# Dilated queries, keys and half of the gate tiles as 2x2 block products in a hybrid encoder layer

## The chip, the core and the metric

The kernel runs on one core of a Trainium2 chip. The core has a matrix engine (TensorE, in the profile PE, with its weight loads as PEld), a vector engine (VectorE, DVE), an engine for activations (ScalarE, ACT), GpSimd (POOL) and SyncE (SP), from whose queue all DMAs of this kernel are issued. Matrix products are summed in PSUM, eight banks of 128 x 512 numbers; all else on the chip lies in SBUF. GpSimd works on SBUF alone. The metric is the device time of one execution in microseconds (us), as the median of several runs; a profile is taken of one execution of its own.

## The reference

One layer of a bidirectional encoder, 1024 tokens of width 1024, all in float32. A normalized input is multiplied by one wide matrix, and the result is cut into the inputs of two attention branches and of their gates:

```python
h = rmsnorm(x, attn_norm_g)
proj = h @ w_in
(c_q, c_kv, k_rope, z_mla, q_dil, k_dil, v_dil, z_dil,
 g_mla, g_dil) = jnp.split(proj, split_points, axis=-1)
a_out = mla_attention(c_q, c_kv, k_rope, positions, mla_q_norm_g, mla_kv_norm_g, w_uq, w_ukv)
y_mla = (a_out * jax.nn.silu(z_mla)) @ w_o_mla
d_out = dilated_mixture(q_dil, k_dil, v_dil, positions)
y_dil = (d_out * jax.nn.silu(z_dil)) @ w_o_dil
gate_mla = jax.nn.sigmoid(g_mla + b_gate[:D_MODEL])
gate_dil = jax.nn.sigmoid(g_dil + b_gate[D_MODEL:])
merged = gate_mla * y_mla + gate_dil * y_dil
return x + merged @ w_out
```

The first branch is latent attention with 8 heads over all keys. The second has three groups of 8 heads with dilations 1, 4 and 16; its queries and keys (3 x 512 columns of `w_in` each) are rotated by position, every query sees the keys up to 64 steps of its dilation away, and the groups are mixed by their softmax denominators. A last RMSNorm follows.

## The kernel before

Every large product is made in three passes: each operand is split into a rounded high part and the remaining low part, and `mm3` (lines 67 to 71) issues high x high, high x low and low x high into the same bank. So a product of a 128 x 128 weight tile with 512 tokens is three matmuls. `split` (73 to 76) makes the high part on ACT and the low part on the engine it is given. The input, transposed to channels by tokens, stays in SBUF as `hT_h` and `hT_l` (8 x 128 channels by 1024 tokens), and `R` holds the factor of each token's norm.

The work is staged. First come the latents and, with 256 columns at a time, the dilated values (`dil_v`). Then `dil_qk` computes queries and keys of the dilated branch, once for each of 3 groups, 2 quads of heads and query or key: two tiles of 128 weight columns (first and second halves of four heads' dimensions), for each half of the tokens 2 x 8 x 3 matmuls into two of six banks, then `rope` (four DVE products, one difference and one sum on POOL), high parts on ACT and low parts on POOL, and stores to DRAM by head, component and part. Group 1 stores the tokens rearranged by residue of 4, group 2 by residue of 16.

Attention follows, first dilated (`dil_attention`), then latent (`mla_attention`). Both leave TensorE waiting for softmax, so other products are put between as fillers: `fillers` is a generator in which every step is one `mm3`. It goes through 24 tiles of the branch gates (0 to 7) and merge gates (8 to 23), 16 steps a tile, then the pieces `brd` of the dilated result, the dilated output projection (64 steps), and, as soon as the first three of four pairs of latent heads are done, the latent output projection (3 steps a piece, 16 pieces). `feed(n)` takes n steps on average at its place, the rates are in `FEED`: the first six are for dilated attention, the last two for latent attention, where they stand twice and four times in a double block of queries. Nineteen steps run ahead of attention (`FIRST_FEED`). What the generator has not done of the latent output projection by the end of attention (all pieces not in `early`) is done in `output`, which adds the last pair of heads, merges the two branches, splits the result, loads and splits `w_out`, and multiplies.

The tile framework places the buffers and waits, and orders each engine's instructions by a simulated schedule of its own, in which a filler is held behind the instruction that `feed` names. The lines that matter most here:

```python
            for i in [4, 5, 6, 7, 0, 1, 2, 3, *range(16, 24), *range(8, 16)]:
                w = self.wtile(a["wt"][T_ZM + i])
...
        while todo:
            while todo[0][0] >= self.mla_done:
                yield
...
                        self.feed(FEED[6])
...
                        self.feed(FEED[7])
```

## Time and profile before

| | |
|---|---|
| median of 3 runs | 1328.5 us (1323.28 to 1333.44) |
| the profiled execution's own time | 1329.38 us |
| its span | 1327.2 us |
| TensorE busy | 1272.2 us (96%) |
| VectorE, ScalarE, GpSimd busy | 647.8, 563.5, 455.3 us |
| mean granted TensorE clock | 0.983 |

A line of a group reads: source line, engine, operation, output and inputs by the program's names, their shapes, the count; then the busy time of all and the mean duration of one in ns; then the idle time of the engine before them and what ended it. The duration of a matmul contains its way through the array, in which the next one already runs, so groups of matmuls look longer than the time that they take from the engine. A table by stretches gives the busy time of each engine with the number of its instructions, then the granted clock, the share of the DMA engines and GB/s. A row of the timeline starts with its time in the span and its duration; in brackets stands the idle time before it and what ended that.

### The profile page before, as it was taken

The page shows a single profiled execution, that of the slowest core. Times are in us where ns is not written, and L with a number is a line of the kernel's source. Part 1 is how long each engine was busy: PE and PEld are TensorE (multiplying, and loading weights), DVE is VectorE, ACT ScalarE, POOL GpSimd, SP SyncE. Part 2 cuts the span into 40 slices and gives each one's busy share as a digit, 9 for nine tenths or more (in the row PEclk, how much of TensorE's full clock was granted, in tenths as well). Part 3 has the DMA queues.
Part 4 walks back from the last instruction along what each step waited for, and adds up shares of the span by engine and source line. Part 5 has one row for each costly group of instructions (what it writes and reads, how often), then busy time and mean ns, then how long its engine had stood idle before and what let it go on. Part 6 is the DMA issues. An engine that isn't in the chain of part 4 may idle for free.

```text
span 1327.2 us, 19295 instructions
## 1 busy us (share of the span) xinstructions
PE 1272.2 (96%) x7101; PEld 1106.5 (83%) x7101; DVE 647.8 (49%) x1204; ACT 563.5 (42%) x1102; POOL 455.3 (34%) x302
## 2 busy tenths in 40 slices
...
GB/s 321 225 163 295 194 238 111 144 212 153 112 110 155 134 111 155 159 188 223 192 186 209 200 211 189 173 106 160 95 92 108 104 178 121 61 123 210 128 93 77
DMA packets 128254, 213.04 MB, mean 161 GB/s; under 512 B 36440, under 2 KB 65696, under 8 KB 126304
## 3 DMA queue, kind: packets, MB, share of 16 engines
...
## 4 chain that ended last, share of the span: by engine, by line
PE 69%; DMA 9%; DVE 6%; issue 2%; SPq 1%; ACT 1%; POOL 0%; DVEq 0%; ACTq 0%; POOLq 0%
PE pj L69 17%; PE pj L71 16%; PE pj L70 16%; PE pt L543 4%; PE av L551 2%; PE av L552 2%; PE s_mla L69 2%; PE s_mla L70 2%; PE s_mla L71 2%; DMA s_sd<-av_t 2%; PE pt L642 1%; PE av L663 1%; SPq L65 1%; PE s_ps L698 1%; PE s_ps L634 1%
## 5 line engine op out<-in xcount | busy, mean ns | idle before, releaser
L76 POOL TENSOR_TENSOR w_l<-w_raw,w_h 128x1024 fp32r<-128x1024 f32 (+1 forms) x70 | 167.5, 2396 | 440.3 <-ACT w_h L75 390.3
L69 PE MATMUL pj<-hT_h,w_h 128*128 128x512 f32 x768 | 314.5, 410 | 2.2 <-DVE zg_z L428 2.1
L71 PE MATMUL pj<-hT_h,w_l 128*128 128x512 f32 x768 | 301.9, 393 | 0.0
L70 PE MATMUL pj<-hT_l,w_h 128*128 128x512 f32 x768 | 301.2, 392 | 0.0
L233 DVE TENSOR_TENSOR rope_m<-pj,cs_d 128x512 f32<-128x512 f32 x96 | 61.8, 686 | 241.1 <-PE pj L71 236.5
L76 DVE TENSOR_TENSOR pt_l<-pt,pt_h 128x512 fp32r<-128x512 f32 x192 | 131.4, 686 | 91.5 <-ACT pt_h L75 89.4
L71 PEld LDWEIGHTS pj<-hT_h,w_l 128*128 128x128 f32 x768 | 145.0, 189 | 31.6
L69 PEld LDWEIGHTS pj<-hT_h,w_h 128*128 128x128 f32 x768 | 145.5, 189 | 27.6 <-DVE zg_z L428 3.0
L75 ACT CAST pt_h<-pt 128x512 fp32r<-128x512 f32 x192 | 112.0, 584 | 130.3 <-PE pt L543 62.1
L70 PEld LDWEIGHTS pj<-hT_l,w_h 128*128 128x128 f32 x768 | 145.8, 190 | 24.6
L70 PE MATMUL pj<-w_l,hT_h 128*128 128x256 f32 x384 | 109.1, 284 | 0.0
L71 PE MATMUL pj<-w_h,hT_l 128*128 128x256 f32 x384 | 108.9, 284 | 0.0
L69 PE MATMUL pj<-w_h,hT_h 128*128 128x256 f32 x384 | 108.9, 284 | 0.0
L75 ACT CAST w_h<-w_raw 128x1024 fp32r<-128x1024 f32 (+1 forms) x70 | 72.3, 1034 | 73.9 <-PE pj L70 59.4
L529 DVE TENSOR_REDUCE m_nm<-s_mla 128x1 f32<-128x1024 f32 x64 | 78.0, 1220 | 33.2 <-PE s_mla L71 33.1
L608 ACT ACTIVATE p<-p,d_st 128x256 f32<-128x256 f32 x128 | 64.4, 504 | 58.5 <-DVE d_st L607 58.5
L532 ACT ACTIVATE p<-s_mla,m_nm 128x1024 f32<-128x1024 f32 x64 | 71.8, 1122 | 25.4 <-PE pt L543 18.4
L543 PE MATMUL pt<-consts,p 128*128 128x128 f32 x512 | 79.7, 276 | 1.8 <-ACT p L532 1.8
L69 PEld LDWEIGHTS pj<-w_h,hT_h 128*128 128x128 f32 x384 | 73.7, 192 | 1.1
L70 PEld LDWEIGHTS pj<-w_l,hT_h 128*128 128x128 f32 x384 | 73.7, 192 | 0.8
L71 PEld LDWEIGHTS pj<-w_h,hT_l 128*128 128x128 f32 x384 | 73.5, 191 | 0.7
L607 DVE CUSTOM_DVE_ANT_0 p<-s_ps,masks 128x256 f32<-128x256 f32 x128 | 51.1, 417 | 45.9 <-PE s_ps L635 25.2
...
## 6 DMA issues: line engine op xcount, KB each, us to landing
w_raw<-wt SPq DMA_DIRECT2D x48, 512.0 KB, 4.4
op_b<-s_dq SPq DMA_DIRECT2D x32, 512.0 KB, 8.6
...
w_raw<-wv SPq DMA_DIRECT2D x12, 512.0 KB, 6.3
```

The lines of the kernel that those rows point to most:

```text
L69: mm(out, lh, rh, start=start, stop=False)
L70: mm(out, lh, rl, start=False, stop=False)
L71: return mm(out, ll, rh, start=False, stop=stop)
L75: self.nc.scalar.copy(out=h, in_=raw)
L76: sub.tensor_tensor(out=l, in0=raw, in1=h.bitcast(F32), op=ALU.subtract)
L233: v.tensor_tensor(out=mi, in0=p, in1=tab, op=ALU.mult)
L529: v.tensor_reduce(out=nm[:, hh, qb:qb + 1], in_=s, axis=AX.X, op=ALU.max, negate=True)
L532: nc.scalar.activation(out=p, in_=s, func=AF.Exp, bias=nm[:, hh, qb:qb + 1], accum_out=den[:, hh, qb:qb + 1])
L543: self.anchor = nc.tensor.transpose(pt[:, o:o + 128], P[b2][:, 128 * kc:128 * kc + 128], self.ident)
L551: nc.tensor.matmul(a_out, vv[:, kc], ph[:, s], start=kc == 0, stop=False)
L607: nc.vector.tensor_tensor_reduce(out=p, in0=s, in1=mask, op0=ALU.add, op1=ALU.min, scale=-0.125, scalar=3e38, accum_out=nm)
L608: nc.scalar.activation(out=p, in_=p, func=AF.Exp, scale=-1.0, bias=nm, accum_out=den)
```

## The change

For two tiles of weight columns, the product over 1024 channels and 1024 tokens is cut into 2 x 2 blocks (two column tiles, two halves of the channels, two halves of the tokens) and made with seven block products instead of eight, in Winograd's form of Strassen's scheme. Each block product is 4 x 3 matmuls of 512 tokens.

- `block_sums` loads the input again and makes, once, four sums and differences of its blocks, split into high and low parts (8 tiles of 8 KB per partition, kept until the last product).
- `block_loads`, `block_minus`, `block_operand`: the two raw weight tiles are loaded two pairs ahead; POOL makes four differences of weight blocks in place; each of the seven blocks is split (ACT, POOL) five products ahead of its use (`LEAD`).
- `block_product` adds into four banks a, b, c, d; c, d and a get a second product. `block_steps` says at which product each further step is issued: copies of banks on ACT, sums of banks on DVE in PSUM, then the rotation, now wholly on DVE with the result in PSUM, high parts on ACT, low parts on DVE, and stores by head and half of the tokens.
- `blocks` runs 16 pairs: the 12 of queries and keys, and 4 of the merge gates 8 to 15 at the places that `ZG_PAIRS` gives. Inside `manual_schedule` every engine keeps the order of the source. All eight banks are used, four for each of two pairs in turn.
- The fillers lose the gate tiles 8 to 15, and the last two rates of `FEED` go from 1.1 to 0.7.
- Queries and keys are stored as head, component, row, part, token, with rows of 512 tokens a store; the loads follow this, keys with two DMAs instead of one, and group 1's keys are read in two runs of 128 columns. `wtile` and `dil_v` hold split weights in halves, four buffers instead of two. The multiplication of the rotary tables by `R` and the zero stores move ahead of the block stage.

```diff
-FEED = (1.9, 1.35, 1.2, 1.25, 2, 3, 1.1, 1.1)
+FEED = (1.9, 1.35, 1.2, 1.25, 2, 3, 0.7, 0.7)
+LEAD = 5
+ZG_PAIRS = ((8, 2), (10, 5), (12, 8), (14, 11))
...
+    def block_sums(self, sp, tp):
+        nc, a = self.nc, self.a
+        p = nc.gpsimd
+        self.sh = [sp.tile([128, 4, 512], F32R, name=f"s{i}_h") for i in range(4)]
+        self.sl = [sp.tile([128, 4, 512], F32R, name=f"s{i}_l") for i in range(4)]
+        for kc in range(4):
+            y = {}
+            for i in range(2):
+                for k in range(2):
+                    x = y[i, k] = tp.tile([128, 512], F32, name=f"y{i}{k}", bufs=2)
+                    c = kc + 4 * k
+                    self.dma(x, a["xt"][i, :, c])
+                    nc.scalar.mul(x, x, self.ga[:, c:c + 1])
+            p.tensor_tensor(out=y[1, 1], in0=y[1, 0], in1=y[1, 1], op=ALU.add)
+            p.tensor_tensor(out=y[1, 0], in0=y[0, 0], in1=y[1, 0], op=ALU.subtract)
+            p.tensor_tensor(out=y[0, 0], in0=y[1, 1], in1=y[0, 0], op=ALU.subtract)
+            p.tensor_tensor(out=y[0, 1], in0=y[0, 1], in1=y[0, 0], op=ALU.subtract)
+            for i, x in enumerate((y[1, 1], y[0, 0], y[1, 0], y[0, 1])):
+                self.split(x, self.sh[i][:, kc], self.sl[i][:, kc], nc.vector)
+    def block_loads(self, n, item):
+        raw = [self.raw_pools[n % 2].tile([128, 8, 128], F32, name="w_raw", bufs=2) for _ in range(2)]
+        for i in range(2):
+            self.dma(raw[i], self.a["wt"][item[0] + i])
+        self.blk[n] = {(k, i): raw[i][:, 4 * k:4 * k + 4] for k in range(2) for i in range(2)}
+    def block_minus(self, j, items):
+        n, k = divmod(j, 7)
+        if n < len(items) and k in (2, 3, 4, 6):
+            b = self.blk[n]
+            out, x, y = {2: ((0, 0), (0, 1), (0, 0)), 3: ((0, 1), (1, 1), (0, 1)), 4: ((0, 0), (1, 1), (0, 0)), 6: ((1, 0), (1, 0), (0, 0))}[k]
+            self.nc.gpsimd.tensor_tensor(out=b[out], in0=b[x], in1=b[y], op=ALU.subtract)
+    def block_operand(self, j, items):
+        n, k = divmod(j, 7)
+        if n < len(items):
+            wp = (self.wp, self.wpx)[j % 2]
+            h = wp.tile([128, 4, 128], F32R, name="w_h", bufs=4)
+            l = wp.tile([128, 4, 128], F32R, name="w_l", bufs=4)
+            self.split(self.blk[n][((0, 0), (1, 0), (0, 0), (0, 1), (0, 0), (1, 1), (1, 0))[k]], h, l, self.nc.gpsimd)
+            self.opd[j] = h, l
+    def block_product(self, j, ps):
+        k = j % 7
+        hx = lambda i, c: tuple(x[:, 4 * c:4 * c + 4, 512 * i:512 * i + 512] for x in (self.hTh, self.hTl))
+        act = (lambda: hx(0, 0), lambda: hx(0, 1), lambda: self.s[0], lambda: self.s[2], lambda: self.s[1], lambda: self.s[3], lambda: hx(1, 1))[k]()
+        w = self.opd.pop(j)
+        out = ps["abcdacd"[k]]
+        for kc in range(4):
+            self.mm3(out, w[0][:, kc], w[1][:, kc], act[0][:, kc], act[1][:, kc], k < 4 and kc == 0, k in (1, 4, 5, 6) and kc == 3, skip=True)
+    def block_steps(self, n, item, ps, tp):
+        nc = self.nc
+        v, act = nc.vector, nc.scalar
+        a, b, c, d = (ps[x] for x in "abcd")
+        tmp = {}
+        def copied(i, x):
+            tmp[i] = tp.tile([128, 512], F32, name="st_c", bufs=2)
+            act.copy(out=tmp[i], in_=x)
+        def both():
+            tmp["t"] = tp.tile([128, 512], F32, name="st_t")
+            v.tensor_tensor(out=tmp["t"], in0=d, in1=tmp[1], op=ALU.add)
+        add = lambda x, i: v.tensor_tensor(out=x, in0=x, in1=tmp[i], op=ALU.add)
+        steps = {
+            2: [lambda: copied(0, a)],
+            3: [lambda: add(b, 0)],
+            4: [lambda: copied(1, c)],
+            5: [both],
+            6: [lambda: copied(2, a), lambda: add(a, "t")],
+            7: [lambda: add(c, 2)],
+            9: [lambda: add(d, 2)],
+        }
+        put = lambda k, f: steps.setdefault(k, []).append(f)
+        if item[1] is None:
+            first = item[0] - T_ZM
+            def out(half, i, x):
+                z = tp.tile([128, 512], F32, name=f"rope_m{i}")
+                t = tp.tile([128, 512], F32, name=f"dq_st{i}{half}")
+                self.zg_out(first + i, half, x, z, t)
+            for k, half, i, x in ((8, 0, 0, b), (8, 0, 1, c), (10, 1, 0, d), (11, 1, 1, a)):
+                put(k, lambda half=half, i=i, x=x: out(half, i, x))
+            return steps
...
+        def rope(half, pa, pb):
+            c512 = slice(half * 512, half * 512 + 512)
+            cos, sin = self.cos_d[:, c512], self.sin_d[:, c512]
+            m = []
+            def sines():
+                for i, x in enumerate((pb, pa)):
+                    m.append(tp.tile([128, 512], F32, name=f"rope_m{i}"))
+                    v.tensor_tensor(out=m[i], in0=x, in1=sin, op=ALU.mult)
+            def cosines():
+                for x in (pa, pb):
+                    v.tensor_tensor(out=x, in0=x, in1=cos, op=ALU.mult)
+            def sums():
+                v.tensor_tensor(out=pa, in0=pa, in1=m[0], op=ALU.subtract)
+                v.tensor_tensor(out=pb, in0=pb, in1=m[1], op=ALU.add)
+            return sines, cosines, sums
...
+        def high(half, o):
+            tiles(half)
+            for i in range(2):
+                x, y = views(half, i, o[i])
...
+        def low(half, o):
+            if g < 2:
+                for i in range(2):
+                    x, y = views(half, i, o[i])
+                    v.tensor_tensor(out=y[1], in0=x, in1=y[0].bitcast(F32), op=ALU.subtract)
+        def store(half):
+            for i in range(2):
+                for j in range(4):
+                    x = slice(32 * j, 32 * j + 32)
+                    if g < 2:
+                        self.dma(dst[j, i, :, :, off + 512 * half:off + 512 * half + 512], st[i, half][x])
+                    elif half:
+                        self.dma(dst[j, i, :, 0], st[i, 0][x])
+        r0, r1 = rope(0, b, c), rope(1, d, a)
+        put(7, r0[0])
+        put(8, r0[1])
+        put(8, r0[2])
+        put(9, r1[0])
+        put(10, lambda: high(0, (b, c)))
+        put(10, r1[1])
+        put(11, r1[2])
+        put(11, lambda: low(0, (b, c)))
+        put(12, lambda: high(1, (d, a)))
+        put(12, lambda: store(0))
+        put(12, lambda: low(1, (d, a)))
+        put(13, lambda: store(1))
+        return steps
+    def blocks(self, items, tp, pp):
...
+        places = 7 * len(items)
+        steps, ps = {}, {}
+        for n in range(2):
+            self.block_loads(n, items[n])
+        for j in range(LEAD):
+            self.block_minus(j, items)
+            self.block_operand(j, items)
+        self.block_minus(LEAD, items)
+        with self.tc.manual_schedule():
+            for x in range(1, places + 14):
+                n, k = divmod(x - 1, 7)
+                j = x - 1
+                if j < places:
+                    if k == 0:
+                        ps[n] = {c: pp.tile([128, 512], F32, name=f"st_{c}{n % 2}") for c in "abcd"}
+                        steps[n] = self.block_steps(n, items[n], ps[n], tp)
+                    self.block_product(j, ps[n])
+                todo = []
+                for m, y in ((n, k + 1), (n - 1, k + 8)):
+                    if m in steps:
+                        todo += steps[m].pop(y, [])
+                for f in todo:
+                    f()
+                self.block_operand(j + LEAD, items)
+                self.block_minus(j + LEAD + 1, items)
+                if k == 2 and n + 2 < len(items):
+                    self.block_loads(n + 2, items[n + 2])
...
-            for i in [4, 5, 6, 7, 0, 1, 2, 3, *range(16, 24), *range(8, 16)]:
+            for i in [4, 5, 6, 7, 0, 1, 2, 3, *range(16, 24)]:
...
-            self.dma(q[rows], self.dq[g][h].rearrange("p c r t -> (c r) p t"))
-        self.dma(k[:, :S + pad], self.dk[g][h].rearrange("a c r t -> (a c r) t"))
+            self.dma(q[rows], self.dq[g][h].rearrange("c r p t -> (c r) p t"))
+        for p in range(2):
+            self.dma(k[64 * p:64 * p + 64, :S + pad], self.dk[g][h].rearrange("c r p t -> p (c r) t")[p])
...
-                qs = slice(128 * b, 128 * b + 128)
-                ks = slice(128 * b, 128 * b + 256) if g == 0 else slice(256 * u, 256 * u + 256)
+                if g == 0:
+                    qs, kb = slice(128 * b, 128 * b + 128), k[:, 128 * b:128 * b + 256]
+                else:
+                    qs, kb = slice(512 * i + 128 * u, 512 * i + 128 * u + 128), k[:, :S].rearrange("p (x r m) -> p r x m", x=2, r=4)[:, u]
...
-            self.dq = [dt(f"s_dq{g}", (8, 2 if g < 2 else 1, 2, 32, S), F32R if g < 2 else F32) for g in range(3)]
+            self.dq = [dt(f"s_dq{g}", (8, 2, 32, 2 if g < 2 else 1, S), F32R if g < 2 else F32) for g in range(3)]
...
-                                for quad in range(2):
-                                    self.dil_v(g, quad, vp, pj)
-                    nc.vector.memset(z, 0.0)
+                            self.dil_v(0, 0, vp, pj)
+                            self.dil_v(0, 1, vp, pj)
+                    sp = sums.enter_context(tc.tile_pool(name="sums", reuse_waits="tile", bufs=1))
+                    with tc.tile_pool(name="bs", reuse_waits="tile", bufs=1) as tp:
+                        self.block_sums(sp, tp)
+                        self.dil_v(1, 0, vp, pj)
+                    for g, quad in ((1, 1), (2, 0), (2, 1)):
+                        self.dil_v(g, quad, vp, pj)
...
+                with tc.tile_pool(name="dt", reuse_waits="tile", bufs=1, side="right") as tp, tc.tile_pool(name="st", reuse_waits="tile", bufs=1, space=PSUM) as pp:
+                    items = [(T_QK + (g * 2 + quad) * 4 + which * 2, g, quad, which) for quad in range(2) for g in range(3) for which in range(2)]
+                    for first, k in reversed(ZG_PAIRS):
+                        items.insert(k, (T_ZM + first, None, None, None))
+                    self.blocks(items, tp, pp)
```

159 lines of the change are left out of this document (77 added, 82 removed).

## The prediction

> **What bounds the kernel now.** I read the busy times and the chain first, then a table of the stages, then the groups.
>
> ```profile
> PE 1272.2 (96%) x7101; PEld 1106.5 (83%) x7101; DVE 647.8 (49%) x1204; ACT 563.5 (42%) x1102; POOL 455.3 (34%) x302
> ...
> PE 69%; DMA 9%; DVE 6%; issue 2%; SPq 1%; ACT 1%; POOL 0%; DVEq 0%; ACTq 0%; POOLq 0%
> ```
>
> TensorE is busy for 1272.2 us of the span's 1327.2 and makes 69% of the chain that ended last. Fewer matmuls are worth time, but only where PE is the limit. The stages are, row by row: dilated queries and keys, dilated attention, latent attention, the merge loop of `output`, the output product.
>
> ```profile
> core 0: us, PE busy (x) PEld busy (x) DVE busy (x) ACT busy (x) POOL busy (x), PEclk, DMA share, GB/s
> 230.60:491.90 261.30, 261.30 (x1155) 216.36 (x1154) 61.83 (x96) 70.32 (x87) 157.81 (x103) 1.00 0.51 140
> 491.90:826.00 334.10, 309.54 (x1839) 269.94 (x1837) 198.53 (x495) 171.67 (x428) 110.15 (x85) 0.97 0.75 195
> 826.00:1187.30 361.30, 352.86 (x2013) 305.18 (x2013) 214.71 (x288) 184.75 (x323) 65.55 (x41) 0.99 0.41 118
> 1187.30:1231.00 43.70, 41.68 (x173) 32.98 (x171) 36.65 (x40) 19.11 (x31) 27.71 (x16) 0.96 0.62 199
> 1231.00:1327.20 96.20, 89.37 (x410) 73.33 (x408) 36.20 (x79) 23.68 (x56) 31.56 (x23) 0.98 0.29 99
> ```
>
> The first row gives the unit of the sum: 1155 matmuls of 512 columns in 261.30 us without idle, **0.2262 us each**. DVE (61.83) and ACT (70.32) have room there.
>
> **What is removed.** A pair of weight tiles over 1024 tokens takes 2 x 2 x 24 = 96 matmuls now, 7 x 12 = 84 as block products. With 12 query/key pairs and 4 pairs of gate tiles, 16 x 12 = 192 matmuls go: 192 x 0.2262 = **43.4 us** of PE, the most that can be gained. But the gate tiles leave the places where they were fillers, so I count by stages.
>
> **The block stage.** 16 x 84 x 0.2262 = 304.0 us against 12 x 96 x 0.2262 = 260.6: **+43.4 us**, if PE never waits. A product lasts 2.71 us, a pair 19.0. Beside it runs, per query/key pair of groups 0 and 1:
>
> ```profile
> L76 POOL TENSOR_TENSOR w_l<-w_raw,w_h 128x1024 fp32r<-128x1024 f32 (+1 forms) x70 | 167.5, 2396 | 440.3 <-ACT w_h L75 390.3
> L233 DVE TENSOR_TENSOR rope_m<-pj,cs_d 128x512 f32<-128x512 f32 x96 | 61.8, 686 | 241.1 <-PE pj L71 236.5
> L76 DVE TENSOR_TENSOR pt_l<-pt,pt_h 128x512 fp32r<-128x512 f32 x192 | 131.4, 686 | 91.5 <-ACT pt_h L75 89.4
> L75 ACT CAST pt_h<-pt 128x512 fp32r<-128x512 f32 x192 | 112.0, 584 | 130.3 <-PE pt L543 62.1
> L75 ACT CAST w_h<-w_raw 128x1024 fp32r<-128x1024 f32 (+1 forms) x70 | 72.3, 1034 | 73.9 <-PE pj L70 59.4
> ```
>
> - DVE: 5 block sums, 12 rotary operations, 4 low parts, 21 x 0.686 = 14.4 of 19.0 us. At most 4 fall on one product (2.74 against 2.71), with 3 or 1 beside it, so a full place catches up.
> - POOL: 7 low parts and 4 weight differences of 512 columns at half of 2.396, 11 x 1.2 = 13.2 us, five products ahead of use.
> - ACT: 3 copies and 11 high parts, 14 x 0.584 = 8.2 us; rearranged ones (group 1) took up to 1.145 (row below), still under 11.
>
> PE stays the limit with 24% of DVE to spare. No row shows DVE writing into PSUM, as most of these operations now do; the nearest rows:
>
> ```profile
> L233 DVE TENSOR_TENSOR rope_m<-pj,cs_d x96: 678/686/694, 231.4 to 487.6; 128x512 f32<-128x512 f32 x96
> L76 DVE TENSOR_TENSOR mg_l<-gate,m 128x512 fp32r<-128x512 f32 x16 | 20.0, 1258 | 1.5 <-ACT m L75 1.2
> L75 ACT CAST dq_st<-rope_m x32: 619/869/1145, 238.9 to 449.2; 128x512 fp32r<-128x512 f32 x32
> ```
>
> With one operand in PSUM an operation took 0.678 to 0.694 us while POOL was busy 60% of the stage; with both in SBUF, beside POOL's adds, 1.258. Every new DVE operation of the stage has a PSUM operand, so I take 0.686; 1.258 is the far end. The Trainium skill ("SBUF — State Buffer", Who interferes with whom) has a rule for it: a VectorE instruction with at most one SBUF input does not contend with GpSimd, one with two does; the two rows agree with it. By that rule the stage stays as summed; with 1.258 for all, DVE needs 21 x 1.258 = 26.4 us a pair, 12 x 7.4 = 89 us more.
>
> The written order adds waits to PE's queue: product 5 adds to the bank of product 1 and waits for ACT's copy of it, 6 for the copy of product 3's bank, 7 for the DVE sum that reads product 4's, and a new pair's first four for the DVE steps of the pair but one before. Behind such a matmul stand all later products. The copies are due two or three products ahead, the DVE sum one (2.71 us, against 0.686 and what is queued ahead of it, at most three operations, 2.1 us); lateness would be paid once a pair, 12 times. I take 0, end 12 x 2.7 = 32 us, which is the place of rival (c).
>
> The sums of input blocks (16 loads, 32 ACT, 16 DVE, 16 POOL operations, at most 32 x 0.6 = 19 and 16 x 1.26 = 20 us on an engine) run beside four of the six value projections: 768 matmuls of 256 columns, at half the unit 87 us. Nothing; up to 10 us if that cover fails.
>
> **Entry and exit.** The block sums hold 64 KB per partition until the last products, and attention's first tiles lie there; the first filler's weights must come too.
>
> ```profile
> w_raw<-wt SPq DMA_DIRECT2D x48, 512.0 KB, 4.4
> op_b<-s_dq SPq DMA_DIRECT2D x32, 512.0 KB, 8.6
> 490.41 3.59 SPq L65 DMA_DIRECT2D s_dk<-dq_st  x8
> ```
>
> The 8.6 us load of queries is covered by the first 19 filler steps, 19 x 3 x 0.2262 = 12.9 us. If the first weights queue on SP behind the last pair's stores (13 DVE operations, 9 us, then 3.6 for eight stores, 4.4 for the load and 3 for its two parts), PE is idle some 20 us. The slot is free long before; I take **+4**, ends 0 and 20. In steady state 16 stores and 2 loads take SP 18 x 0.45 = 8 us of 19; the half stores have five products (13.6 us) before their tile is rewritten: nothing.
>
> **Edits at nothing.** Weights in halves: 0.584 twice for one cast of 1.034, 0.13 us on ACT for some 30 tiles, 4 us beside an ACT that is 42% busy. Keys by two loads of half the size: 16 more issues, under 10 us on SP in 334. Group 1's keys in two runs of 128 columns: the same columns through PE. What they may cost (under 5 us) or save (queries in rows of 8 KB) is in the ends of the exit.
>
> **Latent attention.** Fillers lose 8 tiles x 16 = 128 steps of three matmuls. Dilated attention keeps its rates and, with the first 19, uses 241 steps, of 384 such steps now, of 256 then. Latent attention asked for 192 x 1.1 = 211 steps and now asks for 192 x 0.7 = 134: 15 end the last tile, 64 are the dilated output projection, 21 are empty (the generator waits for the third pair of heads), 34 are the latent output projection, which makes 12 early pieces of it instead of 2. With the pieces finished at the stop, 213 steps become 115: 98 x 3 x 0.2262 = **-66.5 us**, if the rest stays dense.
>
> ```profile
> 826.00:1187.30 361.30, 173.89 (x629) 111.24 (x630) 24.55 (x36) 0.00 (x0) 0.99 0.41 118
> L529 DVE TENSOR_REDUCE m_nm<-s_mla 128x1 f32<-128x1024 f32 x64 | 78.0, 1220 | 33.2 <-PE s_mla L71 33.1
> L532 ACT ACTIVATE p<-s_mla,m_nm 128x1024 f32<-128x1024 f32 x64 | 71.8, 1122 | 25.4 <-PE pt L543 18.4
> ...
> 860.07 0.69 DVE L412 TENSOR_TENSOR zg_z<-zg_z,zg_t 128x512 f32<-128x512 f32 x1 [6.15 <-DMA zg_z<-s_da]
> 861.42 0.39 PE L552 MATMUL av<-pt_l,op_c 128*128 128x256 f32 x1 [2.85 <-DVE pt_l L76]
> ```
>
> The first row counts the stage's filler matmuls, 629 (210 steps), 142 us; without them and 8.4 of idle, one of the 32 double blocks costs PE (361.3 - 142.3 - 8.4) / 32 = 6.6 us. DVE needs 2 x 1.220 + 4 x 0.686 = 5.2 for it, ACT 2 x 1.122 + 4 x 0.584 = 4.6. PE stays the longest even with no filler, with little left to cover a wait. The 21 empty steps leave 5 double blocks bare: 1 us each. Six of the eight pieces `brd` are now made in one burst, their product next in line; one such load held DVE for 6.15 and PE for 2.85 us: 6 pieces cost 0 to 17, I take 6. With 1 for other places, **+12**, ends 0 and 30.
>
> **The merge loop.** Ten pieces fewer are computed there: 10 x 9 x 0.2262 = 20.4 us of PE. But the loop is as much DVE's:
>
> ```profile
> L825 DVE SCALAR_TENSOR_TENSOR gate<-gate,pj x16: 671/675/681, 1200.0 to 1239.4; 128x512 f32<-128x512 f32 x16
> L69 PE MATMUL pj<-wout_h,m x136: 277/394/505, 1231.7 to 1320.3; 128*128 128x512 f32 x120, 128*128 128x256 f32 x16
> ```
>
> Sixteen merges go at 2.6 us each. The output product, 88.6 us dense from 1231.7, follows PE's last piece, though merges run to 1239. With all pieces early or short, half 0 is merged after eight, and its product may start while half 1 merges; but PSUM results leave by DVE, which is full. The gain lies between 0 and 20; **-10**.
>
> **Sum.** 43.4 + 4 - 66.5 + 12 - 10 = -17.1. The profiled execution took 1329.4 (span 1327.2), 0.9 above the median: 1312.3, so **1311** as a median. 1% is 13 us, about what a measurement tells from no change: faster is below 1315, slower above 1342.
>
> **Rivals.** (a) *All cover holds*: entry, bursts and bare blocks free, the merges follow PE: -43.4 + 3, 1288; half-way from the forecast 1299. For: PE has no idle in the first stage; against: DVE's place in the merge loop. 0.17.
>
> (b) *The later stages don't yield*: idle +25 in latent attention, nothing in the merge loop: 43.4 + 4 - 66.5 + 25 = +6, 1335; half-way 1323. For: the 6.15 us wait above; against: 6.6 against 5.2. 0.22.
>
> (c) *DVE bounds the block stage*, the slower side: it decides from 19.0 / 21 = 0.91 us an operation. At 1.03, half more than now for writing PSUM, a pair takes 21.6, 12 x 2.6 = 31 us more: 1342. For: fixed order, one product of slack; against: 0.678 to 0.694. 0.12.
>
> (d) *The clock falls.*
>
> ```profile
> 574.01 0.55 PE L634 MATMUL s_ps<-op_a,op_b 128*128 128x256 f32 x1 [4.60 <-DMA op_b<-s_dq]
> ...
> 579.69 0.63 PE L70 MATMUL pj<-hT_l,w_h 128*128 128x512 f32 x1
> 580.12 0.63 PE L71 MATMUL pj<-hT_h,w_l 128*128 128x512 f32 x1
> ```
>
> After 4.60 us of idle, matmuls came every 0.43 us instead of 0.23. If the five bare blocks ran so, 5 x 6.6 = 33 us more: 1344. "TensorE: Matmul & The Clock Gate" (What's actually happening) of the Trainium skill gives the rule, half clock after an idle window of about 3.4 us. Against: the chain there (1.2 reduce, 1.1 exponential) is shorter, with two score buffers. 0.04.
>
> (e) *The change doesn't do what it says*: the written order also keeps the loads around it back, 20 us at the exit: 1327. 0.05.
>
> **Numbers.** Forecast 0.40, of which 0.28 below 1315. Faster 0.28 + 0.17 + some 0.08 of (b) = 0.53; slower half of (c) and (d), the bad end of (b), 0.12; same 0.35. The range, 1288 to 1337, leaves out the ends of (a), (c) and (d).
>
> **What would show it.** Right: the block stage about 304 us with PE at 100%; latent attention near 307; first output matmul sooner after the last head than now. Wrong: DVE above 0.9 us in the block stage, PE idle after the last product, a latent stage over 325, or an output product that starts no earlier.

## The result: a little slower, not faster

The changed kernel took 1337.31 us (median of 10 runs, 1332.06 to 1342.43) against 1329.62 us of the kernel before beside it (10 runs): a ratio of 1.0065, 95% interval 1.0047 to 1.0083. The forecast was 1311 us, its range 1288 to 1337. By the text's own bound of 1% this is "the same", on the slow side, and the interval leaves out 1; the forecast had it faster. The profiled execution of the changed kernel took 1339.91 us with a span of 1338.1; that of before 1329.38 with 1327.2. The table below therefore explains +10.9 us of span, while the medians are 7.7 us apart: the profiled execution of the changed kernel lies 2.6 us above its median.

The page of the changed kernel, busy times and chain:

```profile
PE 1250.3 (93%) x6909; PEld 1077.0 (80%) x6909; DVE 773.2 (58%) x1388; ACT 623.1 (47%) x1300; POOL 545.6 (41%) x430
...
PE 61%; DMA 15%; DVE 9%; issue 3%; ACT 2%; SPq 1%; POOL 1%; DVEq 0%; ACTq 0%; POOLq 0%
```

The 192 matmuls are gone (7101 to 6909), but TensorE's busy time fell by 21.9 us and not by 43.4, and its share of the chain from 69% to 61% while DMA's rose from 9% to 15%. Where that went is read from the stretches, cut at the first block product, the last one, the first scores of latent attention, the end of its last head, and the first matmul of the output product. First the kernel before, cut the same way, then the changed one (columns: stretch, its length, then busy time and instruction count of each engine, granted clock, DMA share, GB/s):

```profile
225.70:486.30 260.60, 260.60 (x1152) 215.79 (x1151) 60.54 (x94) 69.11 (x84) 159.76 (x102) 1.00 0.51 141
486.30:813.40 327.10, 303.03 (x1800) 264.60 (x1798) 193.62 (x485) 170.63 (x425) 111.71 (x87) 0.97 0.74 193
813.40:1187.30 373.90, 364.96 (x2076) 315.15 (x2077) 220.91 (x299) 188.42 (x329) 66.71 (x42) 0.99 0.43 120
1187.30:1231.70 44.40, 41.92 (x174) 32.99 (x172) 37.35 (x41) 19.11 (x31) 27.71 (x16) 0.96 0.61 196
1231.70:1327.20 95.50, 89.12 (x408) 73.32 (x408) 35.50 (x77) 23.68 (x56) 31.56 (x23) 0.98 0.29 99
```

```profile
226.40:537.10 310.70, 310.70 (x1344) 252.36 (x1345) 168.15 (x266) 127.85 (x236) 223.16 (x175) 1.00 0.53 140
537.10:882.50 345.40, 309.01 (x1798) 268.64 (x1796) 199.26 (x493) 171.66 (x442) 113.89 (x100) 0.95 0.75 191
882.50:1204.10 321.60, 302.04 (x1774) 258.64 (x1772) 214.70 (x292) 172.33 (x315) 63.14 (x52) 0.98 0.45 125
1204.10:1239.20 35.10, 25.07 (x93) 17.69 (x94) 32.16 (x36) 16.26 (x28) 23.69 (x16) 0.94 0.56 184
1239.20:1338.10 98.90, 91.86 (x408) 75.38 (x408) 38.99 (x82) 25.03 (x59) 31.46 (x23) 0.95 0.30 104
```

| stage | measured, us | forecast, us | miss |
|---|---|---|---|
| up to the block stage | +0.7 | 0 | +0.7 |
| block stage | +50.1 | +43.4 | +6.7 |
| exit and dilated attention | +18.3 | +4 | +14.3 |
| latent attention | -52.3 | -54.5 (-66.5 + 12) | +2.2 |
| merge loop and output product | -5.9 | -10 | +4.1 |
| span | +10.9 | -17.1 | +28.0 |

Two rows carry 21 of the 28 us. In the block stage TensorE never stops (310.70 busy of 310.70), and still 1344 matmuls take 0.2312 us each instead of 0.2262. In dilated attention the matmuls are the same (1800 and 1798), but idle time went from 24.1 to 36.4 us and the clock from 0.97 to 0.95, and with it the same matmuls take 6.0 us longer. (In the kernel before, the last head ends at 1186.5, 0.8 us ahead of the cut, so the last two stages are right to 0.8 us only.)

**The block stage.** The timeline of TensorE, the first matmul of each product of one pair (start, duration, instruction):

```profile
306.87 0.39 PE L73 MATMUL st_b<-hT_h,w_h 128*128 128x512 f32 x1
...
309.59 0.40 PE L73 MATMUL st_c<-s_h,w_h 128*128 128x512 f32 x1
...
312.40 0.39 PE L73 MATMUL st_d<-s_h,w_h 128*128 128x512 f32 x1
...
315.20 0.39 PE L73 MATMUL st_a<-s_h,w_h 128*128 128x512 f32 x1
...
318.00 0.39 PE L73 MATMUL st_c<-s_h,w_h 128*128 128x512 f32 x1
...
320.80 0.40 PE L73 MATMUL st_d<-hT_h,w_h 128*128 128x512 f32 x1
```

A product that streams `hT` takes 2.72 us (306.87 to 309.59), one that streams a block sum 2.80 (312.40 to 315.20): 0.2333 us a matmul against 0.2267. Four of the seven products of a pair stream a sum. TensorE doesn't wait for DVE here, whose operations that read and write PSUM took what the prediction had assumed (0.686 us):

```profile
L453 DVE TENSOR_TENSOR st_b<-st_b,st_c x16: 699/700/700, 232.2 to 523.4; 128x512 f32<-128x512 f32 x16
L500 DVE TENSOR_TENSOR st_d<-st_d,cs_d x12: 689/690/692, 252.2 to 540.7; 128x512 f32<-128x512 f32 x12
```

**The exit.** SP's queue around the last product, which ended at 537.1, by the timeline (start, time that the issue took):

```profile
527.85 1.13 SPq L69 DMA_DIRECT2D op_b<-s_dq  x2
...
531.74 2.61 SPq L69 DMA_DIRECT2D op_b<-s_dq  x2
534.54 1.09 SPq L69 DMA_DIRECT2D op_a<-s_dk  x2
...
538.43 4.60 SPq L69 DMA_DIRECT2D w_raw<-wt  x1
543.26 10.94 SPq L69 DMA_DIRECT2D s_dk<-dq_st  x8
556.46 0.36 SPq L69 DMA_DIRECT2D masks<-masks  x1
```

In the kernel before, the loads of the first heads began in the middle of the block stage, the eight stores took 3.59 us to issue, and the masks followed at once:

```profile
L65 SPq DMA_DIRECT2D op_b<-s_dq x48: 573/604/2325, 261.1 to 795.1; - x48
```

```profile
494.10 0.37 SPq L65 DMA_DIRECT2D masks<-masks  x1
```

Now the heads' tiles lie where the block sums were, so ten loads of two heads pile up right before the stores (527.85 to 537.17); the weight load takes 4.60 us to issue and the stores 10.94. TensorE doesn't notice the weights: it goes on with fillers at 537.11. The masks of dilated attention and its zero-padded probabilities (`masks` and `pt0`, in the pool `dx`) lie where the last pair's staging tiles `dq_st` were, and wait for all of that. The waits of DVE and POOL, and TensorE's timeline behind them:

```profile
DVE p L792 <- DMA masks<-masks: 16.8, 1, 16.8
```

```profile
POOL pt_h L1132 <- DMA s_dk<-dq_st: 20.2, 1, 20.2
```

```profile
560.99 0.58 PE L823 MATMUL s_ps<-op_a,op_b 128*128 128x256 f32 x1 [10.42 <-DVE d_st L792]
...
564.14 0.63 PE L75 MATMUL pj<-hT_h,w_l 128*128 128x512 f32 x1
564.57 0.63 PE L73 MATMUL pj<-hT_h,w_h 128*128 128x512 f32 x1
```

TensorE is idle for 10.42 us and then runs with 0.43 us between matmuls of 512 columns until 565.85, 4.9 us from 560.99, where 0.23 us is usual. The Trainium skill ("TensorE: Matmul & The Clock Gate", What's actually happening) has half clock follow an idle window of about 3.4 us and last until a busy one. The trace agrees.

### The profile page after: what moved, and what is told of

The parts are those of the page before. It is cut to its first block, busy times and chain, and to the rows that moved or that the text cites. A ratio compares the mean times of both kernels' runs of the same rounds, so it can differ in the third digit from the quotient of the medians.

```text
span 1338.1 us, 19666 instructions
## 1 busy us (share of the span) xinstructions
PE 1250.3 (93%) x6909; PEld 1077.0 (80%) x6909; DVE 773.2 (58%) x1388; ACT 623.1 (47%) x1300; POOL 545.6 (41%) x430
## 4 chain that ended last, share of the span: by engine, by line
PE 61%; DMA 15%; DVE 9%; issue 3%; ACT 2%; SPq 1%; POOL 1%; DVEq 0%; ACTq 0%; POOLq 0%
PE pj L73 7%; PE pj L74 7%; PE pj L75 7%; PE pt L728 3%; PE st_c L75 2%; PE st_c L74 2%; PE st_c L73 2%; PE st_a L75 2%; PE st_a L73 2%; PE st_a L74 2%; PE st_d L74 2%; PE st_d L75 2%; PE st_d L73 2%; DMA s_sd<-av_t 2%; PE av L737 2%
## 5 line engine op out<-in xcount | busy, mean ns | idle before, releaser
L80 POOL TENSOR_TENSOR w_l<-w_raw,w_h 128x512 fp32r<-128x512 f32 (+1 forms) x188 | 247.3, 1322 | 356.3 <-ACT w_h L79 285.6
L79 ACT CAST w_h<-w_raw 128x512 fp32r<-128x512 f32 (+1 forms) x188 | 113.4, 614 | 137.9 <-POOL w_raw L417 100.6
L73 PE MATMUL pj<-hT_h,w_h 128*128 128x512 f32 x256 | 110.9, 433 | 2.2 <-DVE zg_z L591 2.1
L75 PE MATMUL pj<-hT_h,w_l 128*128 128x512 f32 x256 | 103.3, 404 | 0.0
L74 PE MATMUL pj<-hT_l,w_h 128*128 128x512 f32 x256 | 103.3, 403 | 0.0
L714 DVE TENSOR_REDUCE m_nm<-s_mla 128x1 f32<-128x1024 f32 x64 | 78.0, 1220 | 20.0 <-PE s_mla L75 19.6
L417 POOL TENSOR_TENSOR w_raw<-w_raw 128x512 f32<-128x512 f32 x64 | 84.3, 1317 | 0.0
L737 PE MATMUL av<-pt_l,op_c 128*128 128x256 f32 x256 | 69.5, 295 | 10.0 <-DVE pt_l L80 9.9
L736 PE MATMUL av<-pt_h,op_c 128*128 128x256 f32 x256 | 71.9, 300 | 4.1 <-ACT pt_h L79 3.9
L728 PEld LDWEIGHTS pt<-consts,p 128*128 128x128 f32 x512 | 61.1, 142 | 10.5 <-ACT p L717 4.0
```

Of the source, the lines that this page charges most:

```text
L73: mm(out, lh, rh, start=start, stop=False, skip_group_check=skip)
L74: mm(out, lh, rl, start=False, stop=False, skip_group_check=skip)
L75: return mm(out, ll, rh, start=False, stop=stop, skip_group_check=skip)
L79: self.nc.scalar.copy(out=h, in_=raw)
L80: sub.tensor_tensor(out=l, in0=raw, in1=h.bitcast(F32), op=ALU.subtract)
L417: self.nc.gpsimd.tensor_tensor(out=b[out], in0=b[x], in1=b[y], op=ALU.subtract)
```

## Experiments

Theory: the saved matmuls are real, and were given back at the exit (one queue), in the block stage (the place or the data of the sums), and in cover (filler work that keeps TensorE busy while it would wait) that the gate tiles no longer give. Every run below stands against runs of the kernel before on the same chip; ratios are to those, and the changed kernel's own is 1.0065. Times of stages are from one profile each, and these scatter: four of the changed kernels below that leave the exit as it was took 341.4 to 349.5 us for dilated attention (the two paddings, the input's values in the sum tiles, the rate of 1.1). A few us in that stage are therefore read from the ratios.

### What makes the products with a sum slower

**32 bytes of padding.** As the framework places them (the profile doesn't show places), the sums start at 1856 bytes of a partition, a multiple of 64; `hT` at 139232, 32 past one.

```diff
-        t = cp.tile([128, 1], F32, name="warm")
+        t = cp.tile([128, 9], F32, name="warm")[:, 0:1]
```

> One tile of 32 bytes more ahead of everything on the left side of the SBUF; nothing else. All left tiles, the block sums among them, then start at an odd multiple of 32 bytes, as the token tiles hT do now (sums at 1856 = 29 x 64 bytes, hT at 139232 = 2175.5 x 64). In the changed kernel the products that stream a sum tile are spaced 0.2333 us a matmul, those that stream hT 0.2266. Theory A (where a moving operand starts within 64 bytes sets the spacing): the block stage falls from 310.7 to about 304.6 us, and other matmuls that stream left tiles fall to 0.2266 too, in all 10 us or more off 1337. Theory B (something else sets it: the data, the neighbours, the place in the written order): the stage stays at 310.7 and the time at 1337, within 3.

Measured: 1338.17 us, ratio 1.0063 (1.0037 to 1.0089); block stage 311.6 us, products with a sum still at 2.80. The remainder of 64 isn't it.

**`hT` in the place of the sums.** `block_product` takes quarters of `hT` for all seven products.

```diff
-... lambda: self.s[0], lambda: self.s[2], lambda: self.s[1], lambda: self.s[3], ...
+... lambda: hx(0, 0), lambda: hx(0, 1), lambda: hx(1, 0), lambda: hx(1, 1), ...
```

> The four products that stream a sum tile stream quarters of hT in its place, the sums are made and not used: queries, keys and eight gate tiles come out other than they should, the work is the same in number and size. Theory A or C (the tile streamed sets the spacing, by its place or by its data): the block stage falls from 310.7 to about 304.6 us, all products at 0.2266. Theory B (the place in the written order, or what the other engines do to the banks meanwhile): products three to six stay at 0.233 and the stage at 310.7. By the way: the sums' space comes free before the stage, so the first heads can load early; by the exit theory the 10.42 us of idle after the last product shrink too.

Measured (one run): 1326.88 us. All products take 2.72 us, the block stage 306.4. So it is the tile that is streamed, not the place in the written order or the engines beside. The exit gained as well, as the loads could go early: the longest idle there is 4.21 us, and the stage 339.2 us in place of 345.4.

**The input's values in the sum tiles.** The four additions and subtractions of `block_sums` are left out.

```diff
-            p.tensor_tensor(out=y[1, 1], in0=y[1, 0], in1=y[1, 1], op=ALU.add)
-            p.tensor_tensor(out=y[1, 0], in0=y[0, 0], in1=y[1, 0], op=ALU.subtract)
-            p.tensor_tensor(out=y[0, 0], in0=y[1, 1], in1=y[0, 0], op=ALU.subtract)
-            p.tensor_tensor(out=y[0, 1], in0=y[0, 1], in1=y[0, 0], op=ALU.subtract)
```

> The sums of input blocks are left out: the four sum tiles hold the four quarters of the input themselves, that is the values of hT, in the place of the sums. Queries, keys and eight gate tiles come out other than they should; everything else in the block stage is as in the changed kernel. Products that stream a sum tile take 2.80 us, those that stream hT 2.72. If the data set it (values of sums against values of the input), they fall to 2.72 and the stage by about 5 us; if the place of the tiles sets it, they stay at 2.80.

Measured (one run): 1335.42 us, block stage 310.6 us. The same rows as above:

```profile
309.25 0.39 PE L73 MATMUL st_d<-s_h,w_h 128*128 128x512 f32 x1
312.05 0.39 PE L73 MATMUL st_a<-s_h,w_h 128*128 128x512 f32 x1
```

2.80 us with the values of `hT`: the data isn't it, the place is.

**The sums higher up**, at 45024 to 110560 bytes.

```diff
-tc.tile_pool(name="dvp", reuse_waits="tile", bufs=3, side="right") as vp
+tc.tile_pool(name="dvp", reuse_waits="tile", bufs=3) as vp
-sp = sums.enter_context(tc.tile_pool(name="sums", reuse_waits="tile", bufs=1))
+sp = sums.enter_context(tc.tile_pool(name="sums", reuse_waits="tile", bufs=1, side="right"))
```

> The block sums lie at 45024 to 110560 bytes of a partition (just under the tables and the tokens hT) in place of 1856 to 67392, the staging tiles of the pairs below them. If the distance of a moving tile from the bottom sets the spacing of its products, those that stream a sum fall from 2.80 towards 2.72 us, all or those whose tiles lie highest, and the block stage from 310.7 to 305 to 308. If something else about these tiles sets it, they stay at 2.80. The exit is also another one, since the first heads' tiles now lie where the staging tiles were; by the exit theory it has an idle stretch of 5 us or more.

Measured (one run): 1333.89 us.

```profile
309.90 0.39 PE L73 MATMUL st_d<-s_h,w_h 128*128 128x512 f32 x1
312.62 0.39 PE L73 MATMUL st_a<-s_h,w_h 128*128 128x512 f32 x1
```

All products at 2.72 us, the block stage 304.6, as the forecast's unit gives (304.0). The distance isn't it either, since the ranges of the two cases overlap between 45024 and 67392. What the tiles at 2.72 us share is where they start within 2048 bytes: `hT` and these sums at 2016, those at 2.80 at 1856 and, padded, 1888. (The exit was worse here: 8.95 us of idle on a key load, as those tiles now lay on the staging tiles.)

**160 bytes of padding**, so that everything on the left starts 160 bytes later and the sums at 2016.

```diff
-        t = cp.tile([128, 1], F32, name="warm")
+        t = cp.tile([128, 41], F32, name="warm")[:, 0:1]
```

> 160 bytes more ahead of everything on the left side, nothing else: the block sums start at 2016, 2016 bytes past a multiple of 2048 as hT does (68 x 2048 - 32). Theory (the place within 2048 bytes sets the spacing): products that stream a sum fall from 2.80 to 2.72 us and the block stage from 310.7 to 305 us, latent attention and the output product, which stream left tiles too, lose a few us more, in all 6 to 12 us off 1337. Rival (another property of the place, such as which tiles are its neighbours): 2.80 as before, time within 3 of 1337.

Measured: 1334.16 us, ratio 1.0029 (1.0012 to 1.0045).

```profile
311.42 0.39 PE L73 MATMUL st_d<-s_h,w_h 128*128 128x512 f32 x1
314.14 0.39 PE L73 MATMUL st_a<-s_h,w_h 128*128 128x512 f32 x1
```

2.72 us; the block stage takes 306.3 us, 1.4 of them one wait in the first product. The whole kernel gains 0.36% by the two ratios, 4.8 us, less than the 6 to 12 expected: latent attention, which streams left tiles too, stayed within a us of the 321.6 before it, and dilated attention with its exit took 349.5. That the start within 2048 bytes decides is what these places say (2.72 us at 2016, 2.80 at 1856 and 1888); whether the period is 2048 or a divisor of it from 256 up, they don't.

**The same padding in the kernel before** (the same line of `constants`).

> The kernel before the change with the 160 bytes of padding alone. Its block stage streams hT only and stays at 260.6 us. Left tiles streamed elsewhere: 384 score matmuls and 384 output matmuls of 512 columns, and those of the dilated projection, some 1000 x 0.0067 = 6 us at most, where TensorE is the limit: 1323 to 1328 by the theory of the place, 1329 to 1332 if the place doesn't matter there.

Measured: 1329.91 us, ratio 0.9985 (0.9969 to 1.0002): no difference that can be told from none. The output product went from 95.5 to 94.1 us, the median duration of its matmuls with `m` from 394 to 389 ns; latent attention stayed within a us. The 6 us that the expectation allowed the theory didn't come: by total time the place doesn't matter in that kernel.

### What holds TensorE at the exit

**Masks and padded probabilities where the sums lay**, with the later tiles on the staging tiles, and a pool of its own for latent attention.

```diff
-with ... "op" ... as self.op, ... "ap" ... as ap:
-    with ... "dx" ... as dx, ...
+with ... "op" ... as self.op:
+    with ... "dx" ... as dx, ... "ap" ... as ap, ... "bq" ... as self.bq, ... "np" ... as self.np, ...
...
-    with ... "brd" ... as bp, ...
+    with ... "brd" ... as bp, ... "ap2" ... as ap, ... "np2" ... as self.np, ...
```

> The tiles of dilated attention in another order in the SBUF: masks and the zero-padded probabilities where the block sums lay, the sums of heads (num) and the factor tiles (bc) where the last pair's staging tiles lay; latent attention gets its own pool for p, so that nothing else is shared differently. Block stage, rates and order of work as in the changed kernel. Theory (the exit: TensorE's 10.42 us of idle and the half clock behind it come from the masks, which wait for the last pair's stores, and those for the heads' loads): the masks are issued ahead of the stores, the idle after the fillers shrinks to under 3 us, and 10 to 14 us go, to 1323 to 1327. Rival (the DMA engines are full there whatever the order: loads of two heads, 1 MB of stores, a weight tile): the wait moves to another tile, the first scores or the first transposes, and under 4 us go, 1333 or more.

Measured: 1359.44 us, ratio 1.0216 (1.0188 to 1.0244). The masks' place was free, yet SP still issued them at 552.14, behind the stores, and the idle there was 7.48 us. What made it slow stands at the start of latent attention, behind the new pools: TensorE waited 27.1 us in one piece for the first probabilities, and the reduction they need stood on DVE behind the combination of the last dilated pair. The run says of the theory only that the masks, issued behind the stores, came late although their place was free.

**Staging tiles in a pool of their own**, so that the masks' place comes free early, and SP issues them ahead of the stores.

```diff
+tc.tile_pool(name="dts", reuse_waits="tile", bufs=1, side="right") as self.dts
-st[i, half] = tp.tile([128, 2, 512], F32R, name=f"dq_st{i}{half}")
+st[i, half] = self.dts.tile([128, 2, 512], F32R, name=f"dq_st{i}{half}")
```

> One edit to the changed kernel: the pairs' staging tiles (dq_st) get a pool of their own, so that the place of the masks and of the padded probabilities (pt0) is covered before by weight and rope tiles, which come free some 10 us sooner, and the load of the masks stands ahead of the last pair's eight stores on SP. Theory (the masks' place behind those stores is what leaves TensorE idle for 10.42 us after the fillers and at half clock for 5 us behind that): the masks land by 548, the idle falls to under 4.5 us, dilated attention with its entry from 345 to 333 to 337 us, the time to 1325 to 1330. Rival (the heads' loads fill the DMA engines anyway): idle of 7 us or more, time within 4 us of 1337.

Measured: 1336.47 us, ratio 1.0042 (1.0012 to 1.0071). The idle fell from 10.42 to 4.14 us, the stage to 342.1, short of the theory's 333 to 337. The masks were issued at 546.07, still behind ten loads and a weight tile whose issue took 5.33 us. Of the 6.3 us of idle saved there only 3.3 are left in the stage, since the same matmuls took 312.5 us in this profile after 309.0, and the interval of the ratio overlaps that of the changed kernel: a gain in time isn't shown.

**The second head's loads behind the masks**, on top of that.

```diff
+        with self.tc.issue_after(self.masks_load.ins) if h + g == 1 and hh else ExitStack():
             for rows in (slice(0, 64), slice(64, 128)):
                 self.dma(q[rows], ...)
```

> The changed kernel with the staging tiles apart (as in the earlier run) and the second head's five loads queued behind the masks on SP, so that 2.2 MB of loads stand behind the masks and the last stores, not ahead of them. Theory (the exit is a jam of loads in one queue): the masks land before the first scores, the idle after the fillers falls from 4.1 us to under 1.5, dilated attention with its entry from 342 to 333 or less, the time to 1326 to 1330. Rival (the second head then waits for its loads as long as the first did for the masks): 1334 or more.

Measured: 1331.61 us, ratio 1.0000 (0.9975 to 1.0025). The queue and the stage:

```profile
535.47 0.43 SPq L1128 DMA_DIRECT2D masks<-masks  x1
542.01 3.83 SPq L69 DMA_DIRECT2D s_dk<-dq_st  x8
545.94 1.09 SPq L69 DMA_DIRECT2D op_b<-s_dq  x2
```

```profile
535.80:871.30 335.50, 307.58 (x1797) 266.95 (x1797) 198.94 (x493) 171.93 (x442) 114.14 (x100) 0.96 0.78 197
```

The masks are issued before the last product ends, the eight stores take 3.83 us to issue again, and nothing waits for the masks. In these two profiles the stage takes 335.5 us in place of 345.4; by the ratios the two edits together give 0.65% of the whole, 8.6 us, and the intervals don't overlap. The time ended above the 1326 to 1330 expected: a part of the wait moved, and one of 3.35 us for the second head's keys is the longest now. So the masks' wait at the exit was a jam in one queue, and clearing it gives back some 9 of the 18.3 us.

**More fillers ahead of the first head** (31 steps in place of 19), in the kernel with staging tiles apart and the gate tiles as fillers.

```diff
-FIRST_FEED = 19
+FIRST_FEED = 31
```

> Gates as fillers, staging tiles apart, rate 1.1, and 31 filler steps ahead of the first head in place of 19: 12 x 3 x 0.227 = 8.2 us of the same PE work stand where TensorE was idle for 7.74 us behind the masks. Theory (that idle is lost work, which any filler covers): the longest wait at the exit falls under 2 us and 1315.5 becomes 1305 to 1311, since the half clock behind it goes too. Rival (loads end later whatever covers them, the wait comes back at the second head or as missing cover in latent attention): 1313 or more.

Measured: 1337.42 us, ratio 1.0042 (1.0020 to 1.0064), after 0.9898 without it. My theory failed here in its premise: the first scores stood 6.8 us behind the last product as before, so the steps asked for didn't come ahead of them.

```profile
PE s_ps L823 <- DMA op_a<-s_dk: 15.6, 6, 5.7
PE s_ps L823 <- DVE d_st L792: 14.5, 4, 8.6
```

The stall stayed (8.6 us), and dilated attention waited more for key loads, 15.6 us after 5.6. With 23 matmuls more the stage took 362.6 us after 345.8. Why the loads came later the run doesn't show.

### What the fillers were worth

**Only the query and key pairs as block products**, the eight gate tiles fillers as before, rate 1.1; then the same with the staging tiles apart.

```diff
-ZG_PAIRS = ((8, 2), (10, 5), (12, 8), (14, 11))
+ZG_PAIRS = ()
-            for i in [4, 5, 6, 7, 0, 1, 2, 3, *range(16, 24)]:
+            for i in [4, 5, 6, 7, 0, 1, 2, 3, *range(16, 24), *range(8, 16)]:
```

> Only the 12 query and key pairs are block products; the eight gate tiles are fillers again, with the old rate of 1.1 in latent attention. PE work falls by 12 x 12 x 0.2262 = 32.6 us in the block stage against the kernel before the change. Theory (what is lost is lost at the exit, 14 us, and in the spacing, 0.007 us for 48 of 84 matmuls of a pair, 4 us): 1329 - 32.6 + 14 + 4 = 1315, better than the changed kernel, since latent attention keeps its cover. Rival (work that leaves the fillers or the block stage is lost to other waits whichever way): 1330 or more.

Measured: 1324.93 us, ratio 0.9968 (0.9940 to 0.9995).

> The edit of the staging tiles together with the gate tiles as fillers and the rate of 1.1 (only the 12 query and key pairs as block products). With the gates as fillers alone dilated attention with its entry took 356.4 us, 29 more than before the change, of which 13.2 were one idle stretch behind the masks. Theory: that stretch and the half clock behind it go, 10 to 16 us, to 1309 to 1315. Rival: the 29 us lie elsewhere, in the denser queue of loads, and under 5 us go, 1320 or more.

Measured: 1315.52 us, ratio 0.9898 (0.9874 to 0.9921). With the exit still at 13.21 us of idle in the first of them and 7.74 in the second, three quarters of the pairs already beat both kernels, the first by little. The first missed its 1315 by 10 us; its dilated attention took 356.4 us.

**The rate of latent attention back at 1.1**, in the changed kernel.

```diff
-FEED = (1.9, 1.35, 1.2, 1.25, 2, 3, 0.7, 0.7)
+FEED = (1.9, 1.35, 1.2, 1.25, 2, 3, 1.1, 1.1)
```

> The changed kernel with the rate of fillers in latent attention back at 1.1 from 0.7, nothing else: the same PE work, the steps of the dilated output projection asked for sooner, more empty steps while the third pair of heads isn't done, and all 16 early pieces of the latent projection before the stop in place of 12. By the prediction's terms a bare double block is PE-bound (6.6 against 5.2 us) and pays 1 us; 0.4 x 192 = 77 steps more are asked, of which 12 go to the four pieces and the rest are empty, some 15 more bare double blocks: +10 to +15 us, less 5 from a shorter merge loop: 1342 to 1347. Rival (bare blocks cost nothing, since the order has slack): 1332 or less.

Measured: 1363.68 us, ratio 1.0252 (1.0216 to 1.0288), over 16 us above the range expected.

```profile
884.20:1232.00 347.80, 317.49 (x1816) 272.54 (x1816) 218.87 (x297) 172.43 (x312) 68.14 (x54) 0.97 0.43 118
```

Latent attention took 26.2 us more: 42 more matmuls (9.5 us), idle 30.3 us after 19.6, and 6 us from the clock (0.97 after 0.98). Idle and clock, 16.7 us, are 1.1 us for each of the 15 bare double blocks more, about what the prediction priced. What the expectation had left out is that the earlier pieces cost their matmuls here, while the merge loop and the output product gave only 4 us back.

**Rates and mixtures on top of 31 steps**, staging tiles apart. These two carry the shift that the run above showed to be harmful, and say little else.

```diff
-FEED = (1.9, 1.35, 1.2, 1.25, 2, 3, 0.7, 0.7)
+FEED = (1.9, 1.35, 1.2, 1.25, 2, 3, 0.55, 0.55)
```

and, for the mixture, with a rate of 0.9 and gate tiles 12 to 15 as fillers,

```diff
-ZG_PAIRS = ((8, 2), (10, 5), (12, 8), (14, 11))
+ZG_PAIRS = ((8, 3), (10, 9))
```

> The whole change (16 pairs as blocks), staging tiles apart, 31 filler steps ahead of the first head, and 0.55 as the rate in latent attention, so that 12 steps there are empty in place of 21. Theory (what was lost is idle at the exit, bare blocks, and the half clock behind both): 10 to 14 us at the exit and 4 to 8 in latent attention, less some 4 for more pieces in the merge loop: 1317 to 1325, under the kernel before. Rival (no cover is left to move, what is mended in one place is lacking in the next): 1331 or more.

> Two of the four pairs of gate tiles as block products, the other two as fillers; staging tiles apart, 31 steps ahead of the first head, 0.9 as the rate in latent attention, by which no step there is empty. PE work is 2 x 12 x 0.227 = 5.4 us less than with all gates as fillers. If that counts, it ends 3 to 6 us ahead of the run with all gates as fillers and 31 steps; if cover is worth more than the matmuls saved, level with it or behind.

Measured: 1366.25 us, ratio 1.0263 (1.0243 to 1.0282), and 1350.89 us, 1.0148 (1.0118 to 1.0178). The first came out as its rival had it; the second ended 13 us behind the kernel with all gates as fillers and 31 steps, so the matmuls saved counted for less than the cover. Their dilated stages took 357.9 and 357.4 us.

### Together

**The gate tiles as fillers and all three mends** (staging tiles apart, second head behind the masks, 160 bytes): the diffs above, put together.

> All that helped so far: 12 pairs as blocks with the gates as fillers (rate 1.1, 19 steps ahead), staging tiles apart, the second head's loads behind the masks, 160 bytes of padding. From 1315.5: 6 to 10 us off at the exit (7.74 idle and the half clock behind it), 4 us off in the block stage and a few later by the padding: 1300 to 1307. By the rivals of the single edits: 1312 or more.

Measured: 1309.78 us, ratio 0.9837 (0.9820 to 0.9855), the best of all: 1.6% faster than the kernel before, and 2.8 us above the range expected. The masks' wait is gone here too, but dilated attention is no shorter: 345.3 us (its row is further down) against 345.8 with the staging tiles alone:

```profile
460.70:806.50 345.80, 309.56 (x1798) 268.53 (x1796) 201.27 (x494) 173.36 (x444) 113.99 (x100) 0.95 0.77 193
```

Its idle fell from 36.2 to 33.2 us, with 8.7 us of waits for keys after 5.6, and its matmuls took 2.6 us longer. So in this kernel the gain of the queue's order isn't seen in the stage.

**The whole change with the same mends**, then with a rate of 0.6 (`FEED[6]` and `FEED[7]`).

> The whole change, 16 pairs as blocks and the rate of 0.7, with all three mends: staging tiles apart, the second head's loads behind the masks, 160 bytes of padding. If the two causes add, 1337 - 6 (exit, from the run with the order) - 4 (place) = 1327, at best 1322. The same mends with the gate tiles as fillers gave 1309.8: if this one stays 12 us or more above that, with less work for TensorE, the difference is the cover that the gate tiles gave in latent attention, and no fault of the exit. If it comes to 1315 or less, the prediction's other terms were right.

> As the run with all three mends, the rate in latent attention 0.6 in place of 0.7: 115 steps asked for in place of 134, some 7 of them empty in place of 21, 9 early pieces in place of 12. Theory (empty steps leave bare blocks, each 1 to 2 us of waits and clock, more than a late piece costs in the merge loop): 4 to 10 us faster than with 0.7. Rival (fewer steps mean less cover everywhere, and three more pieces in the merge loop): 0 to 8 us slower.

Measured: 1328.56 us, ratio 0.9959 (0.9936 to 0.9982); with 0.6 it is 1336.87 us, 1.0029 (1.0006 to 1.0052). Against the run with padding alone (1.0029), the whole change gained 0.70% by the mended exit, much as without padding. At 0.6 the rival held: the time is 8.3 us longer by the medians, and latent attention took 331.0 us after 320.0, for 10 matmuls fewer. These two profiles exaggerate it, since the one with 0.7 is of the fastest of its ten executions, 7.1 us under the median, and the one with 0.6 of the slowest. The stages of the whole change with mends, and of the kernel with the gates as fillers (block stage, dilated attention, latent attention, the rest):

```profile
225.60:530.30 304.70, 304.70 (x1344) 252.33 (x1345) 167.96 (x265) 127.75 (x236) 223.11 (x175) 1.00 0.54 143
530.30:868.50 338.20, 308.04 (x1798) 267.91 (x1797) 199.31 (x493) 172.30 (x442) 114.54 (x100) 0.96 0.78 195
868.50:1188.50 320.00, 301.78 (x1771) 259.05 (x1771) 214.38 (x292) 172.39 (x314) 63.52 (x52) 0.98 0.46 126
1188.50:1319.70 131.20, 115.63 (x504) 93.21 (x502) 70.83 (x117) 41.30 (x87) 54.97 (x39) 0.95 0.39 128
```

```profile
222.00:452.20 230.20, 230.17 (x1008) 190.49 (x1009) 144.57 (x229) 93.34 (x179) 166.97 (x131) 0.99 0.59 149
452.20:797.50 345.30, 312.12 (x1797) 270.64 (x1797) 201.55 (x494) 173.34 (x444) 114.20 (x100) 0.95 0.77 194
797.50:1167.90 370.40, 362.87 (x2073) 313.10 (x2074) 219.37 (x299) 189.49 (x341) 68.61 (x54) 0.99 0.44 121
1167.90:1304.50 136.60, 128.31 (x585) 105.91 (x583) 70.27 (x118) 43.42 (x92) 59.71 (x43) 0.99 0.41 133
```

The first has 46 matmuls fewer (5417 against 5463), worth 10.4 us, and takes 11.6 us more: 64 us of idle against 49, and a lower clock, 0.98 and 0.95 in the last two stages against 0.99. By the ratios the difference is 1.2%, 16 us. That is what the gate tiles as fillers were worth, together with the rate that goes with them; the two weren't parted here.

## Why the prediction was wrong, step by step

- **The block stage, +43.4: a term mis-sized by 6.7 us.** The count was right (16 x 84 matmuls, TensorE at 100%, DVE at 0.69 to 0.70 us), the unit was not: 0.2262 us was measured on `hT` alone and taken for tiles whose place I hadn't looked at. With the sums at 2016 bytes past a multiple of 2048 the stage took 304.6 and 304.7 us (304.0 forecast), or 306.3 with one wait in the first product. By the ratios the place is worth 0.36 to 0.41%, some 5 us. Rival (c) is dead, and the far end of 1.258 us with it: DVE took 0.69 us beside a POOL that was busy 72% of the stage. The rule of the Trainium skill that the prediction named for it ("SBUF — State Buffer", Who interferes with whom) agrees with that.
- **Entry and exit, +4: the step that failed.** The prediction priced one weight load behind the stores, and that load came ahead of them and in time. Of the first heads' loads it said only that 19 filler steps cover them. It overlooked that these loads now fall just ahead of the stores in one queue, because their tiles lie on the block sums, and that the masks and `pt0` lie on the staging tiles: TensorE waited 10.42 us for the masks, and with the queue in order 0.65 to 0.70% of the time, some 9 of the 14.3 us that this row missed came back. Its own end of 20 us contained the result (+18.3 with dilated attention); its chosen value didn't. Rival (e) had the exit late by 20 us, at a chance of 0.05; the loads were held back by the space they need and the queue, rather than by the written order that it named.
- **"Edits at nothing": keys by two loads: open.** With the exit mended, dilated attention still took 335.5, 338.2 and, at the rate of 0.6, 342.6 us, 8 to 16 more than before the change. TensorE's waits there for key loads, before and in the whole change with mends:

```profile
PE s_ps L634 <- DMA op_a<-s_dk: 2.5, 1, 2.5
```

```profile
PE s_ps L824 <- DMA op_a<-s_dk: 10.2, 6, 3.8
```

In the changed kernel without the mends, which has the same half loads, they were 1.6 us in two waits. So the half loads didn't show as waits by themselves; these waits appear with the order that puts the second head's loads behind the masks. No run changed the keys' loads alone.

- **Latent attention, -66.5 + 12: right in sum, less so in its parts.** 302 matmuls went (100 steps; the text had 98), idle rose by 10.7 us (19.6 after 8.9), and the stage lost 52.3 us against 54.5. Where the pieces `brd` are made, TensorE was idle for 4.6 us (6 forecast for six pieces), with no wait over 1.1; the longest waits, 3.66 us at the start of the stage and 4.38 behind a load of the latent result, had no term, so some luck is in the 12. The text's table began this stage at 826.0, 12.6 us after its first scores (813.4), so its sign "near 307" means 319 here (321.6 measured), and its 6.6 us a double block come to 6.9. The term holds at the rate of 0.7: the stage took 26.2 us more at 1.1, and the whole 8.3 us more at 0.6 (in the kernel with mends).
- **The merge loop, -10: nearly right,** -5.9; TensorE was idle there for 10.0 of 35.1 us, DVE busy for 32.2, as the text said. The product started 35.1 us after the last head instead of 44.4, but ran at a clock of 0.95 (0.98 before) and took 3.4 us longer. In other profiles of kernels with this edit it took 95.5 to 98.7 us, so a part of that is scatter.
- **Rivals.** Against the sum, (b) came nearest in time (1335), but for another reason: the later stages did yield.

With exit and place mended, the whole change comes to 0.9959 of the kernel before, the forecast having been 0.986 (1311 of 1329.6). The two terms thus make up 14 of the 26 us by the medians. The cause of the other 12 stays open: in the profile of that kernel most of what is left, 7 us, lies in dilated attention, but that profile is of its fastest execution.
